# A last projection in two blocks of seven products

## The chip, the cores and the metric

One core of one Trainium2 chip runs the whole program. The metric is device time in microseconds (us) of one execution, lower being better. The profiled execution also has a span, from the first to the last instruction.

## The reference, cut to what matters

A two-layer decoder trunk on 512 rows of width 1024. Layer 1 is differential attention, layer 2 is a spatial gating unit of width 2048. Only the end of layer 2 and the final norm bear on the change:

```python
proj = h @ w_in                       # 512x1024 @ 1024x6144: u, v, gate
v = rms_norm(v, v_gain)
y = u * (W_s v + b) * silu(gate)      # 512 x 2048, causal 128x128 W_s per group
x = x + y @ sgu_w_out                 # 512x2048 @ 2048x1024   <- the change
return rms_norm(x, final_norm)
```

## The kernel before

Every large product is computed in three passes: each operand is split into a rounded part `hi` and a remainder `lo` (ScalarE makes `hi`, VectorE subtracts to make `lo`), and hi*hi, hi*lo and lo*hi are accumulated in PSUM.

Layer 2's input projection runs as six blocks, numbered 0 to 5. A block is 512x1024 times 1024x1024, done as a two by two block product in seven products instead of eight (Winograd's form of Strassen's scheme). The left operands (`sides`, seven pairs of hi and lo, 512 KB each in f32) come from the normed rows. The right operands come from four quarters a, b, c, d of the weights (1 MB each, tiles `quarter`): class `Quads` loads them with SyncE's queue (SP), splits them, and forms their sums on the way. Two sums are VectorE subtractions (L360, "b minus d" and "b minus a"), two are DMAs on GpSimd's queue (POOL) that add one quarter onto another: first c += a, then a += d. The second writes what the first reads, so it is issued only when the first has landed. The quarter forms are split two products ahead of their use, into three rotating buffer pairs `hi`, `lo` of the pool `wsp`. Call `quads.work(7*n+i+2)` does this during product i of block n.

Products are numbered 0 to 6. Products 0, 2, 4, 5 accumulate in the two banks `px`, products 1, 3, 6 in the two banks `py`. `product_n` (rows on the output partitions) has 24 matmuls of 512 columns; `product_t` (transposed output) has 48 of 256 columns. Blocks 0 and 1 use `product_n`, blocks 2 to 5 `product_t`. Block 5, the last, multiplies its result into `yT`, the layer's branch output (`times`, L993 and L999); after product 4 ScalarE copies `px` aside (`hold`), since product 5 accumulates on.

After block 5 the projection back is a plain product: `out_half` runs twice, once per 512 output columns, over 16 blocks of 128 in the contraction, 4 row blocks and 3 passes, 384 matmuls of 512 columns in all. Its weights come as eight chunks through `load` and `split` (L112, L129, L130), its left operand is split anew in each half (L267, L268). `residual` adds each finished row block onto the residual rows `xr` (L413) and squares it; `emit` computes the row scale by a Newton iteration, scales and stores. The sum of the last row block, its Newton iteration, scaling and store form the tail.

The program is scheduled at build time: each engine gets a fixed list of instructions, run in order; an engine whose next instruction waits does nothing else. `issue_after` pins some of them.

Of the kernel before, what the change touches and what calls it, by code (L numbers as in the profile page):

```python
# [2 lines left out]

# [1 line left out]

# [45 lines left out]
def build(ctx, tc, x, rel_bias, attn_norm, w_in, lq1, lk1, lq2, lk2, subln, w_out,  # L51
# [14 lines left out]
    def bank(name):  # L66
        return psum.tile([P, S], F32, tag="ps", name=name)
# [5 lines left out]
    def wide_src(w, c, n0):  # L73
        return w[0, c * S:(c + 1) * S, n0:n0 + S].rearrange("(k p) n -> p k n", p=P), [4, S]
# [18 lines left out]
        for c in range(4):  # L93
            chunks.append(wide_src(w_out, c, m * S))
    sgu_at = len(chunks)
    for m in range(2):
        for c in range(4):
            chunks.append(wide_src(sgu_w_out, c, m * S))

    raws, splits = {}, {}  # L100
    limit = [qk_first]
# [99 lines left out]
    def square(r, b, m=None):  # L201

        sl = slice(0, D) if m is None else slice(m * S, (m + 1) * S)
        c = 0 if m is None else m
        drop = yT[:, 10:12, :].rearrange("p k n -> p (k n)") if m is None else junk
        nc.scalar.activation(drop, xr[:, b, sl], AF.Square, accum_out=sq[r][b][:, c:c + 1])
        if c == 0:
            hv[r][b] = const.tile([P, 1], F32, name=f"hv{r}_{b}")

    def row_scale(r, b, halves):  # L210

        rs = small.tile([P, 1], F32, name="rs")
        if halves:
            nc.vector.scalar_tensor_tensor(hv[r][b], sq[r][b][:, 1:2], -0.5 / D, hv[r][b], ALU.mult, ALU.add)
        else:
            half_mean(r, b)
        newton(rs, hv[r][b], 1)
        return rs

    def half_mean(r, b):  # L220
        nc.vector.tensor_scalar(hv[r][b], sq[r][b][:, 0:1], -0.5 / D, -0.5 * EPS, ALU.mult, ALU.add)

    hi_last, hT_last, xs_last = [None], [None], [None]

# [286 lines left out]
    def columns_of(w, n0):  # L511
        def of(name):
            r, c = divmod("abcd".index(name), 2)
            return wide_src(w, r, n0 + c * S)[0]
        return of
# [284 lines left out]
        return [yp.tile([P, 4, S], F32R, tag=t, name=t) for t in ("yh", "yl")]  # L800

    acc = [bank(f"acc{b}") for b in range(NB)]
    quads = Quads(qp, [columns_of(sgu_w_in, n0) for n0 in columns])
# [49 lines left out]


    wst = sp.tile([P, KB, P], F32, name="wst")
    bs_bc = sp.tile([P, KB // 2 * P], F32, name="bs_bc")

    def spread_bias(m):
        src = sgu_b_s.rearrange("o g t -> o (g t)")[:, m * KB // 2 * P:(m + 1) * KB // 2 * P]
# [45 lines left out]
            nc.vector.tensor_tensor(v, of_bank(ps[i]), v, ALU.add)  # L905
            total(v, acc)

    i0 += 8
    assert i0 == sgu_at
    late = []  # L910
    for n in range(BR // D):
        for i in range(7):
# [86 lines left out]
            nc.vector.tensor_tensor(y, v.rearrange("p (j n) -> p j n", n=H), y, ALU.mult)  # L999

    VB = BR // D
    for m in range(2):
        for gates in (True, False):
            n = VB + 2 * m + (not gates)
            final = m == 1 and not gates
            t1 = temp()
            if final:
                t4, t2 = temp(), temp()
            for i in range(7):
                work = quads.work(7 * n + i + 2)  # L1010
                if final and i == 5:
                    limit[0] = len(chunks)
                    load(i0)
                if final and i > 4:
                    work = (split(i0, 2 * (i - 5) + h) for h in range(2))
# [12 lines left out]
                if i == (2 if m == 0 and gates else 1):  # L1028
                    times(gates, m, 0, 0, py, t1)
                if i == 2:  # L1030
                    t2 = t2 if final else temp()
                    hold(t2, px)
                if i == 4:
                    t4 = t4 if final else temp()
                    hold(t4, px)
                    times(gates, m, 1, 1, py, t4)
                if i == 5:
                    times(gates, m, 1, 0, px, temp() if gates else None, False)
                if i == 6:
# [4 lines left out]
    yps = tc.tile_pool(name="yp2", bufs=2)
    yp = yps.__enter__()
    fin = yp.tile([P, D], F32, name="fin", bufs=1)
    nc.scalar.dma_start(fin, final_norm.rearrange("(o d) -> o d", o=1).broadcast_to([P, D]))
    acc = [bank(f"acc{b}") for b in range(NB)]
    run(out_half(i0, 0, hT_store, range(4), acc, residual(2, 0, acc)))
    for b in range(NB):  # L1050
        nc.vector.tensor_tensor(xr[:, b, 0:S], xr[:, b, 0:S], fin[:, 0:S], ALU.mult)
    ov = out[0].rearrange("(b p) d -> p b d", p=P)
    acc = [bank(f"acc{b}") for b in range(NB)]
    last = residual(2, 1, acc)

    def emit(b):
        rs = row_scale(2, b, True)
        nc.scalar.activation(xr[:, b, 0:S], xr[:, b, 0:S], AF.Copy, scale=rs)
        nc.vector.scalar_tensor_tensor(xr[:, b, S:D], xr[:, b, S:D], rs, fin[:, S:D], ALU.mult, ALU.mult)
        for m in range(2):  # L1060
            nc.sync.dma_start(ov[:, b, m * S:(m + 1) * S], xr[:, b, m * S:(m + 1) * S])

    def finish(b):
        add = last(b)
        if b < NB - 2:
            emit(b)
        elif b == NB - 1:
            emit(b - 1)
            with tc.issue_after(add.ins):
                emit(b)  # L1070
# [25 lines left out]
```

## Time and profile before

| what | value |
|---|---|
| device time, median of 3 runs | 912.2 us (909.39 to 914.59) |
| device time of the profiled execution | 909.98 us |
| its span | 908.2 us |
| TensorE busy (PE) | 885.3 us, 97% of the span |
| VectorE busy (DVE) | 645.3 us, 71% |
| ScalarE busy (ACT) | 476.9 us, 53% |
| the chain of work that ended last | PE 82%, DVE 10%, DMA 3%, ACT 3%, issue 1% |
| mean granted TensorE clock | 0.997 of full speed |

Busy time of PE counts pipelined matmuls, so the step from one start to the next says what a matmul costs. DMA times run from issue to landing.

### The profile page before, as it was taken

Reading aid. Unit: us, or ns where it says so; the run is one execution under the profiler, and the core shown is the slowest. Engines: PE = TensorE matmul, PEld = TensorE weight load, DVE = VectorE, ACT = ScalarE, POOL = GpSimd, SP = SyncE. Lnnn points to the kernel's source line nnn. Section 1 sums busy time; section 2 is a strip of 40 time slices with the busy share of each in tenths; the row PEclk is TensorE's granted clock in tenths of the full one; section 3 lists DMA queues with packets and bytes.
Section 4 is the critical chain, followed back from the end, with each engine's and each line's share of the span. In section 5 each row is a group of like instructions: output and inputs, shape, how many; then the busy total and the mean of one; then the engine's idle time right before and its main releaser. Section 6 shows DMA issues by size and latency. Waiting matters only on the chain.

```text
span 908.2 us, 14110 instructions
## 1 busy us (share of the span) xinstructions
PE 885.3 (97%) x5393; PEld 774.6 (85%) x5393; DVE 645.3 (71%) x1399; ACT 476.9 (53%) x1015; POOL 34.4 (4%) x52
## 2 busy tenths in 40 slices
PE   7999999999999999999999999998999999999996
PEld 5878999988888888888788887787999999998884
DVE  6945665447787788688886839857795878685634
ACT  7634555446565565566664526736453444454532
POOL 0000100000000000000000002000100000000000
PEclk9999999999999999999999999999999999999998
DMA  8637755373222332321312615554656464534202
GB/s 286 234 90 210 206 192 105 116 245 95 78 90 83 103 90 83 103 89 40 105 47 82 243 29 131 188 128 151 139 163 139 141 139 140 117 134 149 86 4 93
DMA packets 55828, 115.48 MB, mean 127 GB/s; under 512 B 3965, under 2 KB 20398, under 8 KB 52432
## 3 DMA queue, kind: packets, MB, share of 16 engines
q1 hardware_dynamic: 49120, 79.70, 26.5%
q0 software_dynamic: 5584, 33.56, 15.5%
q10 hardware_dynamic: 1056, 1.32, 0.4%
q8 instruction: 42, 0.69, 0.3%
q14 instruction: 26, 0.21, 0.1%
HBM read 89.36 MB, written 6.33 MB: 105 GB/s over the span
## 4 chain that ended last, share of the span: by engine, by line
PE 82%; DVE 10%; DMA 3%; ACT 3%; issue 1%; SPq 0%; ACTq 0%; DVEq 0%; POOLq 0%
PE px L319 15%; PE py L319 11%; PE psqk L254 6%; PE psqk L256 6%; PE psqk L255 6%; PE acc L273 5%; PE acc L275 5%; PE acc L274 5%; PE psv L480 5%; PE po L732 3%; PE pss L694 3%; DMA quarter<-quarter 2%; PE pa L721 2%; DVE lo L374 2%; PE psy L981 2%; PE px L307 1%
## 5 line engine op out<-in xcount | busy, mean ns | idle before, releaser
L374 DVE TENSOR_TENSOR lo<-quarter,hi 128x1024 fp32r<-128x1024 f32 x126 | 152.8, 1236 | 86.0 <-ACT hi L373 85.6
L373 ACT CAST hi<-quarter 128x1024 fp32r<-128x1024 f32 x126 | 128.9, 1047 | 125.7 <-DMA quarter<-quarter 45.7
L130 DVE TENSOR_TENSOR lo<-raw,hi 128x512 fp32r<-128x512 f32 x144 | 93.5, 687 | 39.4 <-ACT hi L129 39.3
L129 ACT CAST hi<-raw 128x512 fp32r<-128x512 f32 x144 | 81.8, 620 | 54.9 <-PE psqk L255 24.7
L254 PE MATMUL psqk<-hT,hi 128*128 128x512 f32 x256 | 101.7, 397 | 0.0
L256 PE MATMUL psqk<-hT,lo 128*128 128x512 f32 x256 | 99.9, 390 | 0.0
L255 PE MATMUL psqk<-hT,hi 128*128 128x512 f32 x256 | 99.9, 390 | 0.0
L707 ACT ACTIVATE e<-e,nm 128x384 f32<-128x384 f32 (+3 forms) x128 | 70.8, 554 | 47.7 <-DVE nm L704 47.3
L319 PE MATMUL py<-hT,hi 128*128 128x256 f32 x512 | 93.0, 284 | 0.0
L273 PE MATMUL acc<-hi,hT 128*128 128x512 f32 x224 | 88.2, 394 | 0.5 <-DVE on L666 0.5
L274 PE MATMUL acc<-lo,hT 128*128 128x512 f32 x224 | 87.3, 390 | 0.0
L275 PE MATMUL acc<-hi,hT 128*128 128x512 f32 x224 | 87.0, 390 | 0.0
L319 PEld LDWEIGHTS py<-hT,hi 128*128 128x128 f32 x512 | 79.8, 192 | 0.0
L319 PE MATMUL py<-hT,lo 128*128 128x256 f32 x256 | 72.5, 283 | 0.0
L704 DVE CUSTOM_DVE_ANT_0 e<-pss,bias 128x384 f32<-128x384 f32 (+3 forms) x128 | 57.3, 484 | 4.1 <-PE pss L694 3.9
L254 PEld LDWEIGHTS psqk<-hT,hi 128*128 128x128 f32 x256 | 48.1, 188 | 12.9 <-issue 2.6
L268 DVE TENSOR_TENSOR hT<-yT,hT 128x512 fp32r<-128x512 f32 x56 | 37.0, 690 | 29.8 <-PE acc L274 17.4
L256 PEld LDWEIGHTS psqk<-hT,lo 128*128 128x128 f32 x256 | 48.1, 188 | 10.1
L255 PEld LDWEIGHTS psqk<-hT,hi 128*128 128x128 f32 x256 | 48.1, 188 | 9.4
L267 ACT CAST hT<-yT 128x512 fp32r<-128x512 f32 x56 | 33.5, 621 | 41.1 <-PE acc L274 35.2
L360 DVE TENSOR_TENSOR quarter<-quarter 128x1024 f32<-128x1024 f32 x36 | 43.3, 1222 | 11.5 <-DMA quarter<-in_sgu_w_in 10.8
L273 PEld LDWEIGHTS acc<-hi,hT 128*128 128x128 f32 x224 | 42.1, 188 | 10.5 <-issue 1.6
(218 smaller groups left out, 2026.6 us busy)
## 6 DMA issues: line engine op xcount, KB each, us to landing
quarter<-in_sgu_w_in SPq DMA_DIRECT2D x48, 512.0 KB, 5.4
raw<-in_attn_w_in SPq DMA_DIRECT2D x38, 512.0 KB, 4.6
quarter<-quarter POOLq DMA_DIRECT2D x18, 1024.0 KB, 7.5
quarter<-in_attn_w_in SPq DMA_DIRECT2D x24, 512.0 KB, 4.8
raw<-in_attn_w_out SPq DMA_DIRECT2D x16, 512.0 KB, 4.4
raw<-in_sgu_w_out SPq DMA_DIRECT2D x16, 512.0 KB, 4.3
vd<-yT POOLq DMA_DIRECT2D x4, 1024.0 KB, 6.0
v<-vd POOLq DMA_DIRECT2D x4, 1024.0 KB, 5.1
```

Of the source, the lines that this page charges most:

```text
L129: nc.scalar.copy(hi[:, sl], raw)
L130: nc.vector.tensor_tensor(lo[:, sl], raw, hi[:, sl].bitcast(F32), ALU.subtract)
L254: nc.tensor.matmul(ps, lhsT=w.hi[:, k, cs], rhs=hT[0][:, k, :], start=(k == 0), stop=False)
L255: nc.tensor.matmul(ps, lhsT=w.hi[:, k, cs], rhs=hT[1][:, k, :], start=False, stop=False)
L256: nc.tensor.matmul(ps, lhsT=w.lo[:, k, cs], rhs=hT[0][:, k, :], start=False, stop=(k == KD - 1))
L273: nc.tensor.matmul(acc[b], lhsT=yh[:, j, bs], rhs=w.hi[:, j, :], start=(k == 0), stop=False)
L274: nc.tensor.matmul(acc[b], lhsT=yh[:, j, bs], rhs=w.lo[:, j, :], start=False, stop=False)
L275: nc.tensor.matmul(acc[b], lhsT=yl[:, j, bs], rhs=w.hi[:, j, :], start=False, stop=(k == KB - 1))
L319: nc.tensor.matmul(ps[f // 2][:, f % 2 * H:(f % 2 + 1) * H], lhsT=w[x][:, k, f * P:(f + 1) * P], rhs=a[y][:, k, :], start=clear, stop=(k = ...
L373: nc.scalar.copy(hi[:, sl], raw[:, sl])
L374: nc.vector.tensor_tensor(lo[:, sl], raw[:, sl], hi[:, sl].bitcast(F32), ALU.subtract)
L707: nc.scalar.activation(e[f][:, cs], e[f][:, cs], AF.Exp, scale=-1.0, bias=nm[:, col], accum_out=l[:, col])
```

## The change

The plain projection is taken out. Its weights become two more blocks of `Quads`, numbered 6 and 7, one for each half of the contraction. Each is seven `product_n`. Their left operands are made from quarters y11, y12, y21, y22 of `yT` into the same buffers `sides`, as soon as the block before has used them (`left`); two sums there are VectorE subtractions and two are POOL DMAs of 512 KB. The results are added onto `xr`: five of the seven products by VectorE (`onto`), and `px` after products 0 and 2 by ScalarE copies and a POOL DMA that accumulates (`put_onto`). The final norm's squares are taken as the halves finish.

```diff
-    for m in range(2):
-        for c in range(4):
-            chunks.append(wide_src(sgu_w_out, c, m * S))
...
+    blocks = [columns_of(sgu_w_in, n0) for n0 in columns] + [rows_of(sgu_w_out, kb) for kb in range(2)]
+    quads = Quads(qp, blocks)
...
+    def left(kb, i):
+        y11, y12, y21, y22 = (quarter_of(kb, q, half) for half in range(2) for q in range(2))
+        raw = (y11, y12, y11, None, y21, y12, y22)[i]
+        if i == 3:
+            raw = temp().rearrange("p f n -> p (f n)").rearrange("p (k n) -> p k n", n=H)
+            nc.vector.tensor_tensor(raw, y21, y11, ALU.subtract)
+            nc.gpsimd.dma_start(y21, y22, accum_op=ALU.add)
+            yield
+        if i == 2:
+            nc.vector.tensor_tensor(y11, y11, y21, ALU.subtract)
+            nc.gpsimd.dma_start(y12, y11, accum_op=ALU.add)
+            yield
+        part(*sides[i], raw)
+        yield
+    def left_work(kb, i):
+        for j in ([], [0], [1], [], [3], [2], [4])[i]:
+            yield from left(kb, j)
+    def left_rest(kb, i):
+        for j in ([5], [], [6], [], [], [], [])[i]:
+            yield from left(kb, j)
...
             for i in range(7):
                 work = quads.work(7 * n + i + 2)
+                if n == OUT - 1:
+                    work = chain(work, left_work(0, i))
...
+    def onto(c, half, ps):
+        ms = slice(c * S, (c + 1) * S)
+        return [nc.vector.tensor_tensor(xr[:, b, ms], ps[b % 2], xr[:, b, ms], ALU.add)
+                for b in (2 * half, 2 * half + 1)]
+    def put_onto(c, half, ps):
+        t = temp()
+        hold(t, ps)
+        region = xr[:, 2 * half:2 * half + 2, c * S:(c + 1) * S]
+        nc.gpsimd.dma_start(region, t, accum_op=ALU.add)
...
+    for kb in range(2):
+        n = OUT + kb
+        for i in range(7):
+            work = chain(quads.work(7 * n + i + 2), left_rest(kb, i), left_work(1, i) if kb == 0 else ())
+            beside(product_n(py if i in (1, 3, 6) else px, sides[i], quads.forms[n, i], i in (0, 1, 3)), work)
+            if i == 0:
+                put_onto(0, 0, px)
+            if i == 1:
+                onto(0, 0, py)
+                if kb:
+                    first_half(0, 0)
+            if i == 2:
+                put_onto(0, 1, px)
+            if i == 3:
+                onto(1, 1, py)
+            if i == 4:
+                onto(1, 1, px)
+                if kb:
+                    first_half(1, 1)
+            if i == 5:
+                onto(1, 0, px)
+                if kb:
+                    for b in range(2):
+                        emit(b, 1)
+            if i == 6:
+                adds = onto(0, 1, py)
+                if kb:
+                    emit(2, 0)
+                    with tc.issue_after(adds[1].ins):
+                        emit(3, 0)
```

`first_half` squares a finished half row block and multiplies it by the norm's weights; `emit` is as before, with the half that finishes last as a parameter.

## Rows read from the trace of the kernel before

**Rows 1.** Busy times in windows: block 1, block 5, projection back (PE, PEld, DVE, ACT, POOL).
```profile
594.40:638.00 43.60, 41.07 (x186) 33.20 (x186) 28.56 (x30) 23.49 (x40) 1.74 (x2) 1.00 0.54 145
772.40:812.50 40.10, 40.10 (x338) 40.10 (x337) 28.51 (x37) 20.36 (x30) 1.70 (x2) 1.00 0.46 120
812.50:899.40 86.90, 86.90 (x385) 71.81 (x383) 47.21 (x92) 35.65 (x69) 0.00 (x0) 1.00 0.24 79
```

**Rows 2.** PE's waits, 555 to 910 us: total, times, longest.
```profile
PE px L307 <- ACT yT L897: 2.8, 3, 1.7
```

**Rows 3.** Timeline of PE (start, duration): projection's first and last matmul, product starts.
```profile
812.36 0.40 PE L273 MATMUL acc<-hi,hT 128*128 128x512 f32 x1
...
899.20 0.39 PE L275 MATMUL acc<-hi,hT 128*128 128x512 f32 x1
...
800.93 0.28 PE L319 MATMUL px<-s4h,hi 128*128 128x256 f32 x1
```

**Rows 4.** Timeline of PE in block 1: products 0, 2, 4 and 5.
```profile
594.44 0.39 PE L307 MATMUL px<-hi,hT 128*128 128x512 f32 x1
...
606.00 0.39 PE L308 MATMUL px<-lo,s2h 128*128 128x512 f32 x1
...
611.13 0.40 PE L309 MATMUL px<-hi,s2l 128*128 128x512 f32 x1
...
618.67 0.50 PE L307 MATMUL px<-hi,s1h 128*128 128x512 f32 x1 [0.79 <-ACT yT L897]
...
629.51 0.50 PE L307 MATMUL px<-hi,s4h 128*128 128x512 f32 x1 [1.74 <-ACT yT L897]
```

**Rows 5.** Timeline of DVE around the end of block 4: wide and narrow steps.
```profile
766.87 2.36 DVE L360 TENSOR_TENSOR quarter<-quarter 128x1024 f32<-128x1024 f32 x2
769.14 0.69 DVE L999 TENSOR_TENSOR yT<-raw,yT 128x512 f32<-128x512 f32 x1
769.74 2.36 DVE L374 TENSOR_TENSOR lo<-quarter,hi 128x1024 fp32r<-128x1024 f32 x2
```

**Rows 6.** DVE by line in block 5, 772.4 to 812.5 us.
```profile
L374 DVE TENSOR_TENSOR lo<-quarter,hi 128x1024 fp32r<-128x1024 f32 x10 | 12.1, 1223 | 6.4 <-ACT hi L373 6.4
...
L130 DVE TENSOR_TENSOR lo<-raw,hi 128x512 fp32r<-128x512 f32 x6 | 4.0, 688 | 0.6 <-ACT hi L129 0.5
L268 DVE TENSOR_TENSOR hT<-yT,hT 128x512 fp32r<-128x512 f32 x5 | 3.4, 687 | 1.1 <-ACT hT L267 1.1
```

**Rows 7.** Timeline of DVE, products 4 and 5 of block 5.
```profile
802.36 0.68 DVE L130 TENSOR_TENSOR lo<-raw,hi 128x512 fp32r<-128x512 f32 x1
802.96 0.69 DVE L999 TENSOR_TENSOR yT<-raw,yT 128x512 f32<-128x512 f32 x1
```

**Rows 8.** Timeline of POOL: the accumulating DMAs of blocks 1 and 5.
```profile
595.96 0.87 POOL L365 DMA_DIRECT2D quarter<-quarter  x1 [33.36 <-ACT hi L373]
604.17 0.87 POOL L365 DMA_DIRECT2D quarter<-quarter  x1 [7.34 <-DVE lo L374]
...
772.40 0.85 POOL L365 DMA_DIRECT2D quarter<-quarter  x1 [35.24 <-DVE lo L374]
780.31 0.85 POOL L365 DMA_DIRECT2D quarter<-quarter  x1 [7.06 <-issue]
```

**Rows 9.** Timeline of ACT: what it did when the second accumulating DMA landed.
```profile
615.53 1.05 ACT L373 CAST hi<-quarter 128x1024 fp32r<-128x1024 f32 x1 [10.10 <-DMA quarter<-quarter]
616.49 0.63 ACT L900 ACTIVATE junk<-yT 128x512 f32<-128x512 f32 x1
...
788.00 2.00 ACT L373 CAST hi<-quarter 128x1024 fp32r<-128x1024 f32 x2 [7.38 <-DMA quarter<-quarter]
```

**Rows 10.** Timeline of DVE in block 1: a sum, and the split after the landing.
```profile
605.52 0.69 DVE L905 TENSOR_TENSOR yT<-py,yT 128x512 f32<-128x512 f32 x1 [0.92 <-PE py L309]
...
616.61 1.22 DVE L374 TENSOR_TENSOR lo<-quarter,hi 128x1024 fp32r<-128x1024 f32 x1 [9.80 <-ACT hi L373]
```

**Rows 11.** All 18 accumulating DMAs of L365, 1 MB each.
```profile
DMA to landing us min/median/max: 6.9/7.5/11.3
```

**Rows 12.** Timeline of DVE: last sum onto the rows and last scaling.
```profile
900.33 0.68 DVE L413 TENSOR_TENSOR xr<-acc,xr 128x512 f32<-128x512 f32 x1
...
903.59 0.75 DVE L1059 SCALAR_TENSOR_TENSOR xr<-xr,rs,fin 128x512 f32<-128x512 f32 x1
```

More of the change, by code (lines that the diff above doesn't have):

```diff
@@ L2 @@
 from contextlib import ExitStack
+from itertools import chain
 import numpy as np
@@ L206, in square, with row_scale @@
         nc.scalar.activation(drop, xr[:, b, sl], AF.Square, accum_out=sq[r][b][:, c:c + 1])
-        if c == 0:
+        if b not in hv[r]:
             hv[r][b] = const.tile([P, 1], F32, name=f"hv{r}_{b}")
-    def row_scale(r, b, halves):
+    def row_scale(r, b, halves, second=1):
         rs = small.tile([P, 1], F32, name="rs")
         if halves:
-            nc.vector.scalar_tensor_tensor(hv[r][b], sq[r][b][:, 1:2], -0.5 / D, hv[r][b], ALU.mult, ALU.add)
+            nc.vector.scalar_tensor_tensor(hv[r][b], sq[r][b][:, second:second + 1], -0.5 / D, hv[r][b], ALU.mult,
+                                           ALU.add)
         else:
@@ L218, in row_scale, with half_mean @@
         return rs
-    def half_mean(r, b):
-        nc.vector.tensor_scalar(hv[r][b], sq[r][b][:, 0:1], -0.5 / D, -0.5 * EPS, ALU.mult, ALU.add)
+    def half_mean(r, b, m=0):
+        nc.vector.tensor_scalar(hv[r][b], sq[r][b][:, m:m + 1], -0.5 / D, -0.5 * EPS, ALU.mult, ALU.add)
     hi_last, hT_last, xs_last = [None], [None], [None]
@@ L802, in build, with rows_of, of @@
     acc = [bank(f"acc{b}") for b in range(NB)]
-    quads = Quads(qp, [columns_of(sgu_w_in, n0) for n0 in columns])
+    def rows_of(w, kb):
+        def of(name):
+            r, c = divmod("abcd".index(name), 2)
+            return wide_src(w, 2 * kb + r, c * S)[0]
+        return of
+    blocks = [columns_of(sgu_w_in, n0) for n0 in columns] + [rows_of(sgu_w_out, kb) for kb in range(2)]
+    quads = Quads(qp, blocks)
     gen = out_half(i0 + 4, 1, lambda c: (hT_store if c < 2 else yp_store)(c), range(4), acc,
@@ L855, in build @@
     wst = sp.tile([P, KB, P], F32, name="wst")
-    bs_bc = sp.tile([P, KB // 2 * P], F32, name="bs_bc")
+    bs_bc = sp.tile([P, KB // 2 * P], F32, tag="row", name="bs_bc")
     def spread_bias(m):
@@ L906, in plus @@
             total(v, acc)
-    i0 += 8
-    assert i0 == sgu_at
+    assert i0 + 8 == sgu_at
     late = []
@@ L1001, in build, with quarter_of @@
     VB = BR // D
+    OUT = 3 * VB
+    def quarter_of(kb, q, half):
+        return yT[:, 8 * kb + 4 * q:8 * kb + 4 * q + 4, half * H:(half + 1) * H]
+    def left(kb, i):
[18 more added lines that the diff above has]
+            yield from left(kb, j)
     for m in range(2):
@@ L1004, in build @@
             n = VB + 2 * m + (not gates)
-            final = m == 1 and not gates
             t1 = temp()
-            if final:
-                t4, t2 = temp(), temp()
             for i in range(7):
                 work = quads.work(7 * n + i + 2)
[L1011 to L1015, printed above, removed]
+                if n == OUT - 1:
+                    work = chain(work, left_work(0, i))
                 beside(product_t(py if i in (1, 3, 6) else px, sides[i], quads.forms[n, i], i in (0, 1, 3)), work)
@@ L1030, in build @@
                 if i == 2:
-                    t2 = t2 if final else temp()
+                    t2 = temp()
                     hold(t2, px)
                 if i == 4:
-                    t4 = t4 if final else temp()
+                    t4 = temp()
                     hold(t4, px)
@@ L1040, in build @@
                     times(gates, m, 0, 1, py, t2)
+    fin = sp.tile([P, D], F32, tag="row", name="fin")
+    nc.scalar.dma_start(fin, final_norm.rearrange("(o d) -> o d", o=1).broadcast_to([P, D]))
+    ov = out[0].rearrange("(b p) d -> p b d", p=P)
+    def onto(c, half, ps):
[7 more added lines that the diff above has]
+        nc.gpsimd.dma_start(region, t, accum_op=ALU.add)
@@ new lines, in first_half, with emit @@
+    def first_half(m, half):
+        ms = slice(m * S, (m + 1) * S)
+        for b in (2 * half, 2 * half + 1):
+            square(2, b, m)
+            half_mean(2, b, m)
+            nc.vector.tensor_tensor(xr[:, b, ms], xr[:, b, ms], fin[:, ms], ALU.mult)
+    def emit(b, m):
+        square(2, b, m)
+        rs = row_scale(2, b, True, m)
+        o, n = slice((1 - m) * S, (2 - m) * S), slice(m * S, (m + 1) * S)
+        nc.scalar.activation(xr[:, b, o], xr[:, b, o], AF.Copy, scale=rs)
+        nc.vector.scalar_tensor_tensor(xr[:, b, n], xr[:, b, n], rs, fin[:, n], ALU.mult, ALU.mult)
+        for sl in (o, n):
+            nc.sync.dma_start(ov[:, b, sl], xr[:, b, sl])
@@ L1041, in build @@
     scope.__exit__(None, None, None)
     quarters.__exit__(None, None, None)
[L1044 to L1070, printed above, removed]
@@ L1072, in build @@
-    run(out_half(i0 + 4, 1, hT_store, range(4), acc, finish))
-    yps.__exit__(None, None, None)
 _INS = ["x", "rel_bias", "attn_norm", "attn_w_in", "attn_lam_q1", "attn_lam_k1", "attn_lam_q2", "attn_lam_k2",
```

## The prediction

> **What bounds the kernel now.** I read the windows first [rows 1]: in block 5 and in the projection back PE is busy without a gap, at full granted clock, while DVE has 28.5 of 40.1 us and 47.2 of 86.9 us. So at this end of the kernel only fewer matmuls help. Next the list of PE's waits [rows 2]: from 555 us on its longest total is 2.8 us, and every line in it is a `product_n` line of blocks 0 and 1; no `product_t` of blocks 2 to 5 and no matmul of the projection waits. Block 1 is the only steady block of the kind that the change builds, and there PE has 41.1 of 43.6 us. The timelines of PE, POOL, ACT and DVE say why, and the argument stands on them.
>
> **What is removed.** 384 matmuls become 2 x 7 x 24 = 336. The price of one is the step between starts, not its 390 ns: (899.20 - 812.36) / 383 = 0.2267 us [rows 3]. 48 x 0.2267 = **10.9 us saved**. Against it, the products whose side lies in a tile of sums step slower: 22 steps from 606.00 to 611.13 are 0.233 us each [rows 4]. Three of seven products are such: 2 x 72 x 0.0065 = **0.9 us back**.
>
> **What is added off PE.** A wide VectorE operation (128x1024) costs 1.135 us back to back (766.87 to 769.14 for two), a narrow one 0.6 [rows 5]. Block 5 loses 11 narrow ones (L130, L268) [rows 6] and gets 15 wide: two splits of block 6 (4), its subtractions (4), sides 0, 1, 3, 2, 4 (5 remainders, 2 subtractions). 28.5 - 6.6 + 17.0 = 38.9 of 40.1 us. Block 6 has 14 + 4 + 9 wide and 10 narrow operations, 30.6 + 6.0 = 36.6 us in 7 x 5.45 = 38.2 us. So VectorE fits, at 96 to 97%, but only without waiting, and in block 5 its splits alone wait 6.4 us for ACT [rows 6]. I charge nothing for these operations by themselves; their cover is PE's time, and what they cost is lateness, worked out below. ScalarE has room (20.4 us in block 5). The 16 weight loads of 512 KB stay on SP, now into quarters as these come free; the `fin` load stays on ACT's queue, behind nothing new. POOL gets twelve new DMAs: four of 1 MB (quarters), eight of 512 KB (sides and `put_onto`).
>
> **Where PE will wait.** Time 0 is the start of block 6 (812.36). Each block carries c += a, then a += d, then the split for product 4. In block 5 the first was issued at +0.1 after the block's start (772.40; the start is 772.3, seven products of 5.72 us before 812.36), in block 1 at +1.5 [rows 4, 8].
>
> Block 6: VectorE reaches product 5 of block 5 with its `times` free at 803.56, less the one L130 that falls away: -9.4 [rows 7]. Then in its list: split (6,0) 2.3, b - d 2.3, side 2 2.3, `times` 1.2, split (6,1) and b - a 4.5. So c += a is issued at **+3.1**. From one issue to the next it was 8.2 us in block 1 and 7.9 in block 5; the second landed 11.4 us after its issue in block 1, where weight loads ran beside it, and 7.7 in block 5 [rows 8, 9]. All 18 lie between 6.9 and 11.3 [rows 11]. Loads for block 7 run here too: I take 8.2 and 9.5. `put_onto` puts 512 KB into the same queue; the trace has no such transfer, so between 0 and half of 7.5 us, and I take 1, since it is issued when much of c += a has moved. Landing L = 3.1 + 8.2 + 9.5 + 1 = 21.8 (18.3 to 26.4). In block 1 product 4 started 3.1 us after the landing (615.53 to 618.67): 24.9, against 4 x 5.45 + 0.3 = 22.1 due. **2.8 us (0 to 7.4).**
>
> Then product 5 of block 6. It accumulates on `px`, which VectorE must first add onto the rows, behind everything that stood behind the landing: 1.1 to the first remainder [rows 9, 10], split (6,4) 2.3, split (6,5) 2.3, the add of `py` 1.2, split (6,6) 2.3, y21 - y11 1.1, then 0.6 for the first bank: L + 10.9. Product 4 ends at L + 3.1 + 5.45. **2.3 us** (0 if the add goes first; 4.6 if two sides stand there too). Before, a ScalarE copy freed `px` at this point and PE went straight on (800.93 [rows 3]); in block 1, PE waited 1.74 us within product 5 [rows 4].
>
> Block 7: from product 5 of block 6 the list is 1.1 + 0.6 + 2.3 + 2.3 + 2.3 + 1.2 + 4.5 = 14.3 us in 10.9, so c += a is at +3.4. No weights load any more: 3.4 + 7.9 + 7.7 + 1 = 20.0 (18.6 to 23.1), product 4 at 23.1: **1.0 us (0 to 4.1)**. Product 5: as above without y21 - y11, L + 9.8 against L + 8.55: **1.2 us (0 to 3.5)**.
>
> The tail stays: the last bank is added, put through Newton and scaled with the same operations (900.33 to 903.59 [rows 12]), and the banks of the last four row blocks finish 8.2, 5.4, 2.7 and 0 us before the last matmul, as now. Bound: 0.5 us either way, taken as 0.
>
> A 1 MB accumulating DMA takes 7.5 us in the median here [rows 11]. The Trainium skill ("DMA: Bandwidth & Descriptors", section on the anatomy of one DMA on the software path) fits 2.0 us plus bytes over 436 GB/s, which would be an estimated 4.4 us. By it the chain would land at about +12 and neither product 4 would wait, about 7 us better than my sum; the trace disagrees with it for accumulating transfers, so I keep the rows.
>
> **Sum.** -10.9 + 0.9 + (2.8 + 2.3 + 1.0 + 1.2) = -2.7 us. The profiled execution took 909.98 us (span 908.2), so 907.3; the median of the runs is 2.2 above it, so **909.5**. With all waits at their low ends -10.0, at their high ends +9.6. The measurement tells 0.5%, 4.6 us, from no change.
>
> **The rivals.**
> *The chain lands in time (faster).* If VectorE is not late at the end of block 5, c += a goes out at +0.1; with 7.5 and 7.7 us it lands at 15.3, VectorE never stands and none of the four waits appears: -10.0, 902.2. For it: blocks 2 to 5 have the same chain and PE never waits. Against it: there a product takes 5.72 us and not 5.45, and VectorE had room; in block 1 the chain landed at +21.1.
>
> *`put_onto` queues behind the second quarter DMA (slower).* POOL's list is fixed at build. If a += d stands ahead of `put_onto` of product 0, POOL waits for c += a to land, and `put_onto` is issued at 3.1 + 8.2 + 0.9 and lands behind a += d: + 9.5 + 3.8 = 25.5. VectorE's add of `py` waits for that, since both add to the same rows, and product 3 (due at 16.5) needs `py`: 9.6 us; then 2.3 at product 5. In block 7, 3.4 + 7.9 + 0.9 + 7.7 + 3.8 = 23.7, 7.8 us, and 1.2. Together 20.9, so +10.9: 923; with the quicker landings of both 917. It decides if a += d is listed first: `put_onto` is ready at 6.0, a += d only when c += a has landed, but lists made as though DMAs were quick put it first. For it: ACT stood 10.1 us before a split that waited for this very DMA, with a square behind it whose input was ready at 606.2 and which ran at 616.49 [rows 9, 10]. Against it: a += d also needs split (6,2), which VectorE has at about +9.
>
> **How the numbers follow.** My forecast, PE's saving mostly eaten by waits (5.4 to 14.6 us of them), 0.40; its own range is 907.6 to 916.8. The chain in time or nearly so, 902 to 907.6, 0.36: it is well supported by four blocks, and the lateness that I charge is small beside the uncertainty of a fixed order that I infer. Behind the queue, or the waits near their high ends, 0.24. Hence faster 0.36, same 0.40, slower 0.24. The range leaves out about 1 in 10 at each side: 903 to 917.
>
> **What would show it.** PE in blocks 6 and 7: gaps of 1 to 3 us at the starts of products 4 and 5 and none elsewhere. POOL: c += a issued 3 us after each block's start, and `put_onto` before a += d. VectorE: above 90% busy from 772 us on. The matmul step 0.227 to 0.233. I am wrong if c += a goes out near 0 (then faster), if PE stands at the start of product 3 (slower), or if the tail from the last matmul is not 8.8 us.

## The result, and the profile after

The changed kernel takes 924.49 us (median of 4 runs, 921.91 to 927.16), beside 912.29 us for the kernel before on the same chip: a ratio of 1.0136, 95% interval [1.009, 1.0181]. It is slower, and above the range that was given (903 to 917, predicted 909.5). The profiled execution took 922.71 us, with a span of 921.0 us against 908.2.

First where the span grew. These are the windows of the changed kernel, cut at the starts of block 5, 6 and 7 and at the last matmul; the columns are those of [rows 1].

```profile
772.30:821.40 49.10, 42.65 (x338) 42.44 (x337) 35.87 (x38) 23.47 (x28) 4.30 (x4) 0.93 0.63 151
821.40:872.40 51.00, 42.68 (x170) 33.80 (x169) 36.61 (x39) 22.57 (x25) 6.75 (x6) 0.90 0.72 165
872.40:911.80 39.40, 38.86 (x169) 31.28 (x168) 30.79 (x53) 18.61 (x31) 4.20 (x4) 1.00 0.46 94
```

Block 5, whose own matmuls are not changed, takes 49.1 us where it took 40.1 [rows 1]: 9.0 us lost before the new work has begun on TensorE. Block 6 takes 51.0 and block 7 39.4. Together these two take 90.4 us for 87.1 of the plain projection (812.36 to 899.43 [rows 3]): 3.3 us lost. The tail grew by 0.45 us. VectorE, forecast at 96 to 97%, is busy for 36 of 49 and 37 of 51 us.

PE's waits over the same stretch (total, times, longest), which had no entry at all there before [rows 2]:

```profile
PE px L318 <- ACT raw L331: 6.5, 1, 6.5
PE py L306 <- ACT hi L372: 5.1, 1, 5.1
PE px L306 <- DVE xr L1078: 2.7, 2, 2.1
PE py L307 <- DVE lo L373: 1.1, 1, 1.1
```

Together 15.4 us. PE's timeline has them at these places (start, duration):

```profile
807.54 0.58 PE L318 MATMUL px<-s4h,hi 128*128 128x256 f32 x1 [6.45 <-ACT raw L331]
807.92 0.42 PE L318 MATMUL px<-s4l,hi 128*128 128x256 f32 x1
808.14 0.41 PE L318 MATMUL px<-s4h,lo 128*128 128x256 f32 x1
...
812.94 0.28 PE L318 MATMUL px<-s4l,hi 128*128 128x256 f32 x1
813.06 0.28 PE L318 MATMUL px<-s4h,lo 128*128 128x256 f32 x1
...
843.21 0.77 PE L306 MATMUL py<-hi,hT 128*128 128x512 f32 x1 [5.13 <-ACT hi L372]
...
860.43 0.68 PE L306 MATMUL px<-hi,s4h 128*128 128x512 f32 x1 [2.14 <-DVE xr L1078]
```

The rows are product 5 of block 5, product 3 and product 5 of block 6. Block 7 has one wait, of 0.5 us, at product 5. The second to fifth row show what each longer stand costs beside itself: the step after it is 0.22 us and only later 0.12. The row of product 3 names a cast of ScalarE's, which ended at 843.2 and is not an operand of that product; VectorE's add of `py` onto the rows, which frees the bank that product 3 writes, ran from 842.37 (below), its first bank 0.69 us. Four windows of PE (busy, granted clock, DMA share, GB/s) say why the steps are slow: one before the stand, and one behind each of the three stands.

```profile
794.00:801.00 7.00, 7.00 (x60) 1.00 0.98 217
807.50:812.60 5.10, 5.06 (x23) 0.50 0.85 244
843.20:848.50 5.30, 5.29 (x16) 0.65 0.84 186
860.40:864.00 3.60, 3.57 (x9) 0.53 1.08 201
```

Behind the first stand the granted clock is 0.50, the lower of its two levels (1.2 GHz); the last two windows reach past the end of that stretch, and show 0.65 and 0.53. Product 5 of block 5 took 8.12 us for 5.68, and product 3 of block 6 took 7.32 for 5.45. So the three longer stands cost 13.7 us by themselves and some 2 us more each.

What came late? ScalarE behind product 4 of block 5, where `hold` (L331) has to free `px`:

```profile
803.13 1.05 ACT L297 CAST s2h<-yT 128x1024 fp32r<-128x1024 f32 x1 [8.90 <-DVE yT L1022]
804.08 1.99 ACT L372 CAST hi<-quarter 128x1024 fp32r<-128x1024 f32 x2
805.97 1.04 ACT L297 CAST hT<-raw 128x1024 fp32r<-128x1024 f32 x1
806.92 0.57 ACT L331 COPY raw<-px 128x512 f32<-128x512 f32 x1
```

Side 2 of block 6 stands ahead of `hold` in ScalarE's list, and it waits 8.9 us for VectorE's y11 - y21 (L1022). VectorE's timeline shows what that waited for, and the same kind of wait at four other places:

```profile
789.50 1.23 DVE L373 TENSOR_TENSOR lo<-quarter,hi 128x1024 fp32r<-128x1024 f32 x1 [4.55 <-ACT hi L372]
...
801.87 1.23 DVE L1022 TENSOR_TENSOR yT<-yT 128x1024 f32<-128x1024 f32 x1 [4.87 <-DMA yT<-yT]
...
842.37 1.29 DVE L1078 TENSOR_TENSOR xr<-py,xr 128x512 f32<-128x512 f32 x2 [7.24 <-DMA xr<-raw]
...
855.14 1.22 DVE L1022 TENSOR_TENSOR yT<-yT 128x1024 f32<-128x1024 f32 x1 [3.73 <-DMA yT<-yT]
...
884.94 0.69 DVE L1078 TENSOR_TENSOR xr<-py,xr 128x512 f32<-128x512 f32 x1 [2.63 <-DMA xr<-raw]
...
913.09 0.68 DVE L1078 TENSOR_TENSOR xr<-py,xr 128x512 f32<-128x512 f32 x1
...
916.36 0.75 DVE L1100 SCALAR_TENSOR_TENSOR xr<-xr,rs,fin 128x512 f32<-128x512 f32 x1
```

The last two rows are the tail, which runs as before [rows 12]. POOL's timeline has the issues (against [rows 8]):

```profile
780.19 0.86 POOL L364 DMA_DIRECT2D quarter<-quarter  x1 [6.82 <-issue]
795.41 1.29 POOL L1019 DMA_DIRECT2D yT<-yT  x1 [14.37 <-PE py L318]
...
822.13 0.89 POOL L364 DMA_DIRECT2D quarter<-quarter  x1 [17.20 <-DVE quarter L359]
...
830.31 0.86 POOL L364 DMA_DIRECT2D quarter<-quarter  x1 [7.28 <-issue]
830.86 1.53 POOL L1085 DMA_DIRECT2D xr<-raw  x1
...
879.05 1.20 POOL L1085 DMA_DIRECT2D xr<-raw  x1 [3.29 <-ACT raw L331]
882.46 0.91 POOL L364 DMA_DIRECT2D quarter<-quarter  x1 [2.21 <-DVE lo L373]
```

Read with VectorE's rows: y21 += y22 (L1019) is issued at 795.41, and L1022, which reads y21, goes on at 801.87, 6.5 us later. In block 6, c += a is issued 0.7 us after the block's start, a += d at 830.31, and `put_onto` right behind it. VectorE's add of `py` onto the same rows goes on at 842.37, 11.5 us after that. In block 7 the order is the other way round, and VectorE goes on 5.9 us after `put_onto`'s issue. The medians from issue to landing, over the whole run (against [rows 11]):

```profile
quarter<-quarter POOLq DMA_DIRECT2D x22, 1024.0 KB, 7.6
...
yT<-yT POOLq DMA_DIRECT2D x4, 512.0 KB, 6.4
xr<-raw POOLq DMA_DIRECT2D x4, 512.0 KB, 5.4
```

Half the bytes take 5.4 to 6.4 us, not half the time.

### The profile page after: what moved, and what is told of

Read it like the earlier page. It is cut to its first block, busy times and chain, and to the rows that moved or that the text cites. A ratio compares the mean times of both kernels' runs of the same rounds, so it can differ in the third digit from the quotient of the medians.

```text
span 921.0 us, 14023 instructions
## 1 busy us (share of the span) xinstructions
PE 882.3 (96%) x5345; PEld 769.6 (84%) x5345; DVE 673.3 (73%) x1401; ACT 486.1 (53%) x1001; POOL 48.2 (5%) x64
## 5 line engine op out<-in xcount | busy, mean ns | idle before, releaser
L373 DVE TENSOR_TENSOR lo<-quarter,hi 128x1024 fp32r<-128x1024 f32 x154 | 186.0, 1233 | 91.4 <-ACT hi L372 91.0
L372 ACT CAST hi<-quarter 128x1024 fp32r<-128x1024 f32 x154 | 156.8, 1047 | 146.0 <-DMA quarter<-quarter 50.8
L128 DVE TENSOR_TENSOR lo<-raw,hi 128x512 fp32r<-128x512 f32 x112 | 73.0, 688 | 39.0 <-ACT hi L127 39.0
L127 ACT CAST hi<-raw 128x512 fp32r<-128x512 f32 x112 | 64.0, 621 | 48.4 <-PE psqk L254 24.8
L359 DVE TENSOR_TENSOR quarter<-quarter 128x1024 f32<-128x1024 f32 x44 | 52.9, 1221 | 9.6 <-DMA quarter<-in_sgu_w_in 9.4
L253 PEld LDWEIGHTS psqk<-hT,hi 128*128 128x128 f32 x256 | 48.1, 188 | 12.8 <-issue 2.6
L255 PEld LDWEIGHTS psqk<-hT,lo 128*128 128x128 f32 x256 | 48.1, 188 | 10.1
L306 PE MATMUL py<-hi,hT 128*128 128x512 f32 x112 | 44.8, 400 | 5.8 <-ACT hi L372 5.1
L318 PEld LDWEIGHTS py<-hT,lo 128*128 128x128 f32 x256 | 49.1, 192 | 0.0
L307 PE MATMUL py<-lo,hT 128*128 128x512 f32 x112 | 44.5, 397 | 1.1 <-DVE lo L373 1.1
L308 PE MATMUL py<-hi,hT 128*128 128x512 f32 x112 | 44.5, 397 | 0.0
L479 PE MATMUL psv<-hi,hT 128*128 128x512 f32 x128 | 41.8, 404 | 0.5 <-ACT hT L240 0.5
L364 POOL DMA_DIRECT2D quarter<-quarter x22 | 19.5, 888 | 397.6 <-DVE lo L373 216.1
```

What stands on the lines that cost most here:

```text
L127: nc.scalar.copy(hi[:, sl], raw)
L128: nc.vector.tensor_tensor(lo[:, sl], raw, hi[:, sl].bitcast(F32), ALU.subtract)
L253: nc.tensor.matmul(ps, lhsT=w.hi[:, k, cs], rhs=hT[0][:, k, :], start=(k == 0), stop=False)
L255: nc.tensor.matmul(ps, lhsT=w.lo[:, k, cs], rhs=hT[0][:, k, :], start=False, stop=(k == KD - 1))
L306: nc.tensor.matmul(ps[i], lhsT=a[0][:, k, rs], rhs=w[0][:, k, :], start=(start and k == 0), stop=False, **more)
L318: nc.tensor.matmul(ps[f // 2][:, f % 2 * H:(f % 2 + 1) * H], lhsT=w[x][:, k, f * P:(f + 1) * P], rhs=a[y][:, k, :], start=clear, stop=(k = ...
```

## Experiments

Two theories were tried against each other. By the first (A, called A2 and A3 in later runs, as each expectation states it), the loss is engines that stand in a fixed list for a DMA, the work queued behind them, and the slow clock behind each stand of PE. By the second (B), the loss is that VectorE has no room for the new work. "The kernel" below is the changed one; times are medians, ratios are to the kernel before, run beside it. Rows and block times are those of the one profiled execution, and diffs are cut to the line that matters.

**Which DMA.** The two sums of the left sides, or `put_onto` of `px`, or both, become VectorE adds.

```diff
-            nc.gpsimd.dma_start(y21, y22, accum_op=ALU.add)
+            nc.vector.tensor_tensor(y21, y21, y22, ALU.add)
...
-            nc.gpsimd.dma_start(y12, y11, accum_op=ALU.add)
+            nc.vector.tensor_tensor(y12, y12, y11, ALU.add)
```

> The two POOL DMAs of each block's left sums (y21 += y22, y12 += y11) become VectorE additions, four wide operations of 1.14 us more in all. Theory A (an instruction that waits for a POOL DMA stands in VectorE's and ScalarE's fixed lists ahead of the add or copy that frees px): the 6.45 us gap at product 5 of block 5 and its slow matmuls (2.4 us) go, and so does most of the 5.4 us lost in products 5 and 6 of block 6; the 5.1 us gap at product 3 of block 6 stays, since it belongs to the sum onto the rows. 14 us less than the changed kernel: 908 to 912 us. Theory B (VectorE is full, 96%, and its lateness is what PE waits for): 4.6 us more work on VectorE, so no gain or a loss, 922 to 929 us.

917.87 us, 1.0056 [1.0037, 1.0074]: 6.6 us of the 12 come back, but in the profiled execution not in block 5. It still takes 49.1 us, while the loss at products 5 and 6 of block 6 is gone (45.9 us). PE's first wait there:

```profile
PE px L318 <- ACT raw L331: 6.6, 2, 6.0
```

The list order (side 2 and a split ahead of `hold`) is unchanged, and the chain of the quarters was later in this run: a += d, issued at 784.03 beside the weight loads of block 6, had ScalarE waiting until 794.80, 10.8 us. So block 5 has two sources of lateness that feed one list, and taking one away left the other. In the changed kernel's profile the same DMA let ScalarE go on 8.2 us after its issue (780.19 to 788.42). The profiled execution of e1, though, is the longest of ten (920.95), and PE had stood 1.3 us in block 4 already, which the edit does not touch; no profile shows block 5 in a shorter one. The plain form of theory A, one wait behind one gap, did not come out here.

```diff
-                put_onto(0, 0, px)
+                onto(0, 0, px)
...
-                put_onto(0, 1, px)
+                onto(0, 1, px)
```

> px of products 0 and 2 is added onto the rows by VectorE instead of a ScalarE copy and a POOL DMA, eight narrow operations of 0.6 us more on VectorE. Theory A: only the gap at product 3 of block 6 (5.1 us and 1.9 us of slow matmuls) goes, the gap at product 5 of block 5 stays: 915 to 919 us. Theory B: 4.8 us more on VectorE, 922 to 929 us.

924.04 us, 1.0095 [1.0063, 1.0127]. The gap at product 3 of block 6 goes (block 6 43.0 us), but block 5's gap grows to 9.7 and block 7 takes 44.1. This profile too is of the longest of seven executions (926.82; three took 918.3 to 918.6), in which ScalarE again went on 10.8 us after the issue of a += d.

> Both of the above. Theory A: all three losses go, 20 us less than the changed kernel, 902 to 906 us, faster than the kernel before. Theory B: 9.4 us more VectorE work, 925 to 934 us.

918.33 us, 1.0059 [1.0031, 1.0088]. Block 6 42.2, but block 5 50.1 with a gap of 6.0, and block 7 44.6 with waits for VectorE at products 1, 4 and 5. The profile is of the longest of eight executions (924.97; five took 915.4 to 919.7); here ScalarE went on 11.1 us after a += d's issue. In it each wait removed is partly given back by another.

**An earlier issue.** y21 - y11 and the DMA behind it move from product 4 to product 1.

```diff
-        for j in ([], [0], [1], [], [3], [2], [4])[i]:
+        for j in ([], [3, 0], [1], [], [3], [2], [4])[i]:
```

> The same work as the changed kernel on every engine, but y21 - y11 and the DMA y21 += y22 are issued in product 1 instead of product 4; only the remainder and cast of side 3 stay in product 4. Theory A: the DMA has landed long before its sum is wanted, so the gap at product 5 of block 5 and the wait for y21 in block 6 go: 908 to 913 us. Theory B: VectorE's work is the same, so the time is that of the changed kernel, 921 to 927 us.

924.13 us, 1.0118 [1.0094, 1.0141]. Block 5 falls to 44.8 us, its gap to 2.6 (now within product 4), so this DMA is indeed part of its loss. It was issued 14.4 us earlier in the block, 0.6 us behind a += d, and VectorE went on only 6.7 us earlier, after a wait of 10.3. Block 6 gets a gap of 10.75 at product 3: there the early DMA is issued at 834.16, right behind a += d (832.90) and `put_onto` (833.45), and three transfers are in flight on the queue at once.

**The order of the lists.** `issue_after` pins the work of product 5 behind `hold` (block 5) and behind VectorE's add of `px` (blocks 6 and 7); nothing else changes.

```diff
-                beside(product_t(...), work)
+                with tc.issue_after(freed[0].ins) if n == OUT - 1 and i == 5 else ExitStack():
+                    beside(product_t(...), work)
```

> The same operations, transfers and sizes as the changed kernel; only the lists' order differs: ScalarE's work of product 5 in block 5 is put behind the copy of px of product 4, and VectorE's work of product 5 in blocks 6 and 7 behind the add of px of product 4. With that the sum of px onto the rows also comes ahead of the second quarter DMA in POOL's list of block 6. Theory A2 (the order of the lists is at fault: work that belongs to product 5 stands ahead of the copy that frees px, and put_onto behind a DMA that waits 8 us): block 5 falls from 49.1 us to 41 to 43, the gap at product 3 of block 6 (5.1 us and 1.9 us of slow matmuls) goes, and what is left in block 6 is the wait at product 4 for the two quarter DMAs, some 3 us. In all 906 to 914 us. Theory B (VectorE's and POOL's amount of work sets the pace): the work is the same, so the wait moves to another product: 920 to 927 us.

924.87 us, 1.0126 [1.0079, 1.0172]. Block 5 falls to 43.0 us and the gap at its product 5 is gone, which shows that the list order carries that gap. The time does not move: PE now stands 2.15, 3.71 and 2.3 us in block 6, each time with a product of about 7.2 us behind it, and block 7 takes 43.6 us.

> Only POOL's list is changed: in blocks 6 and 7 the sum of px of product 0 onto the rows is issued before the second quarter DMA. Theory A2: the gap at product 3 of block 6 (7 us with its slow matmuls) becomes a shorter one at product 4, since the quarter DMA now comes later (3 us); block 5 stays at 49 us: 918 to 922 us. Theory B: no change, 921 to 927 us.

Here POOL's list has `put_onto` of product 0 ahead of a += d:

```diff
-                put_onto(0, 0, px)
+                put = put_onto(0, 0, px)
+                with tc.issue_after(put.ins):
+                    quads.add(n, "a", "d")
```

927.25 us, 1.0154 [1.0123, 1.0186]. The gap at product 3 is gone, so the queue order made it; but later VectorE stands for the left side's sum with everything behind it, and PE for VectorE at product 6. The row of VectorE, with its wait:

```profile
858.56 1.22 DVE L1022 TENSOR_TENSOR yT<-yT 128x1024 f32<-128x1024 f32 x1 [9.97 <-DMA yT<-yT]
```

PE's gap behind it is 11.74 us, the longest of all runs.

**Pins with one kind of DMA gone.**

> The pins of e5_pin, and the left sums by VectorE instead of POOL (four wide operations, 4.6 us, more on VectorE). Theory A2: block 5 as in e5_pin, and no instruction waits for a 512 KB sum of the left side any more; the loss of 5.4 us in products 5 and 6 of block 6 goes as it did in e1_left_dve: 904 to 911 us. Theory B: 4.6 us more than e5_pin.

917.23 us, 1.0045 [1.0012, 1.0078]: as without the pins (e1), within the intervals.

> The pins of e5_pin, and px of products 0 and 2 added onto the rows by VectorE (eight narrow operations, 4.8 us, more on VectorE; no DMA onto the rows). Theory A2: no product waits for a DMA onto the rows, 2 to 4 us less than e5_pin: 904 to 911 us. Theory B: up to 4.8 us more than e5_pin.

916.61 us, 1.0051 [1.0007, 1.0095]. With the gap of block 5 and `put_onto` out of the way, the longest wait left is at the place that the prediction worked out, product 4 of block 6, with a partner in block 7:

```profile
PE px L306 <- DVE xr L1081: 4.0, 1, 4.0
...
PE px L306 <- ACT hi L373: 1.9, 1, 1.9
```

c += a went out 5.6 us after the block's start, a += d 7.6 us later, and ScalarE went on behind its landing at +21.5. But what PE waited for is VectorE's add of `px` after product 2, which this run itself put into VectorE's list behind the split that waited for the landing. By the prediction's own 3.1 us from landing to start, product 4 would have stood some 0.6 us.

**All the new DMAs, one kind, or VectorE's work left out.** e9 drops the twelve new accumulating DMAs, e10 those of blocks 6 and 7's quarters alone, e11 the fourteen remainders of the left sides. The diff is e11's.

```diff
-        part(*sides[i], raw)
+        nc.scalar.copy(sides[i][0], raw)
```

> Leaves out all twelve new accumulating DMAs: the quarter sums of blocks 6 and 7, the two left sums of each, and the sums of px of products 0 and 2 onto the rows. PE, ScalarE and VectorE keep every instruction. Theory A3 (waits for POOL DMAs, in whichever order the lists stand, make nearly all of PE's gaps): blocks 5 to 7 fall from 139.4 us to 118 to 124 us, PE's work alone being 117: 901 to 909 us, faster than the kernel before. Theory B (VectorE has 96% of the time to fill, so any order leaves PE waiting for it): VectorE's work is the same, blocks 5 to 7 stay above 132 us: 915 to 924 us.

904.38 us, 0.992 [0.9891, 0.9949]. Its blocks 5, 6 and 7, in windows as above:

```profile
773.00:813.00 40.00, 40.00 (x338) 40.00 (x337) 32.73 (x36) 23.61 (x28) 1.70 (x2) 1.00 0.58 159
813.00:855.30 42.30, 40.71 (x170) 32.53 (x170) 40.49 (x42) 22.68 (x25) 0.00 (x0) 0.96 0.28 100
855.30:894.10 38.80, 38.77 (x169) 31.35 (x168) 30.32 (x55) 19.21 (x31) 0.00 (x0) 1.00 0.04 14
```

All the work of PE, ScalarE and VectorE is there, in the same list order in block 5 (side 2 is still cast ahead of `hold`), and block 5 takes its 40.0 us without a gap. VectorE has 40.5 of 42.3 us in block 6 and PE waits 1.6 us in all. In block 5 c += a and a += d are still DMAs, and VectorE still waits 4.53 us for the split behind them; only the left sides' DMAs are gone there. So with the new DMAs gone the order does no harm, VectorE's work fits (103.5 us in the three blocks, for 103.3 in the changed kernel), and the loss comes from these DMAs: from the waits for them, by the rows above, though this run takes their traffic away too.

> Leaves out only the four quarter DMAs of 1 MB in blocks 6 and 7. Theory A3: put_onto has POOL's queue to itself, the gap at product 3 of block 6 goes (7 us with its slow matmuls), block 5 keeps its gap of 6.4 us, and products 5 and 6 of block 6 keep their wait for y21: 914 to 919 us. Theory B: 921 to 927 us.

922.41 us, 1.0129 [1.0077, 1.0181]: the chain of the quarters alone is not it. Block 5 keeps its gap (6.4), the one at product 3 of block 6 goes, and PE stands 6.2 us for VectorE at product 6 of block 6, where VectorE waits 8.6 us for y21 += y22.

> Leaves out VectorE's fourteen remainders of the left sides (15.9 us of its work, in blocks 5, 6 and 7); the matmuls read old values. All DMAs and ScalarE casts stay. Theory A3: the gap at product 5 of block 5 stays (it waits for the DMA y21 += y22) and so does the one at product 3 of block 6: 915 to 922 us. Theory B: with 16 us less for VectorE the gaps go: 902 to 910 us.

921.81 us, 1.0118 [1.0083, 1.0153]. Taking 15.9 us of work from VectorE moves the ratio by 0.002; gaps of 4.7, 4.6 and 3.4 us remain, and VectorE is busy for 92.5 of 140 us. Theory B falls, as the cause of this kernel's loss. It falls by e9 and e11, and not by the ranges as such: A's ranges came out in e9 and e11 alone so far, the times of e2, e4, e5 and e10 lie in B's, and those of e1, e3, e6, e7 and e8 in neither, since A took each cure to be worth a whole gap and another wait took its place.

**A version without the waits.** VectorE adds c += a in blocks 5 to 7 (below), y21 += y22 (not in e14), and `px` onto the rows after product 0 (in e12 and e14 after product 2 as well), with the pins of e5. As DMAs stay y12 += y11, a += d, and in e13 one `put_onto` for each block.

```diff
-                self.add(n, "c", "a")
+                for h in range(2):
+                    sl = slice(2 * h, 2 * h + 2)
+                    nc.vector.tensor_tensor(c[:, sl], c[:, sl], a[:, sl], ALU.add)
```

> The pins, and four kinds of POOL DMA replaced by VectorE operations so that none of them stands in front of a fixed list: y21 += y22 of each half (2 wide operations in all), px of products 0 and 2 onto the rows (8 narrow), and the first quarter sum c += a of blocks 5, 6 and 7 (6 wide), so that the second, a += d, is issued at once and no longer 8 us later. 13.8 us more for VectorE. The same result as the reference. Theory A3: blocks 5 to 7 at 119 to 126 us against 133.4 with the pins and the sums of px on VectorE alone: 900 to 908 us. Theory B, or that the pins were not the cause: VectorE has 123 us of work for 117 us of PE: 914 us or more.

914.51 us, 1.0019 [1.0, 1.0037]. Block 5 is 40.05 us, but the time lies in theory B's range, and so does the next run's.

> As e12_chain, but px of product 2 goes onto the rows by ScalarE and a POOL DMA, since nothing reads those rows before product 6: 2.4 us less for VectorE, two more DMAs of 512 KB. Theory A3: within 2 us of e12_chain, or better by up to 2 us: 899 to 908 us. Theory B: 912 us or more.

913.31 us, 1.0009 [0.9991, 1.0026].

> As e12_chain, but y21 += y22 stays a POOL DMA. It tells the quarter chain from the left sums. Theory A3: VectorE waits 4 to 5 us for y21 in block 5 and as long in block 6; some 4 to 8 us more than e12_chain: 905 to 914 us. If it is no slower than e12_chain, the left sums cost nothing once the quarter chain is short.

915.95 us, 1.0029 [1.0014, 1.0044], not to be told from e12: with c += a quick and the pins in place, what the wait for y21 costs is within the noise, and not the 4 to 8 us that were expected. e13's ratio is 1.0009 for 1.0136, with the same products: eleven of the twelve microseconds came back with these waits, but none of the saving is left over, since the adds are now VectorE's work. What PE stands for now is VectorE, at product 1 of block 7 in e13 for 4.1 us, with the two halves of c += a listed ahead of the add that frees `py`. The next two move these adds behind it, with the pins and without.

> As e13_chain_p0 (blocks 40.1, 43.9, 45 us; 913.3 us), but in blocks 6 and 7 VectorE's two adds of c += a are listed behind the add that frees py in product 0, not ahead of it. Theory A2 (what is left over the saving is PE standing for work that waits in an engine's list behind other work, and the slow product after each longer stand): the gap of 4.14 us at product 1 of block 7 and the 1.9 us of its slow product go, and the 1.79 us at product 1 of block 6: 7.8 us less, 905 to 907 against a before of about 912. Rival (VectorE has no slack left in these blocks, so that lateness moved in one place comes back in the next): the gaps come back at products 3 to 5, and the time stays at 912 to 914.

911.36 us, 0.9984 [0.9969, 0.9999]: below the rival's range by 0.6 us and far above A2's.

> As e15_late_c without the pins (the sides and splits of product 5's successors may stand ahead of the step that frees px). Theory A2: with nothing of VectorE's list waiting for a DMA the order does little harm: block 5 within 1 us of e15's, the whole within 3 us of e15. Rival (the order itself is what costs): block 5 has a gap of 2 us or more at product 5 and the whole is 4 us or more above e15.

910.51 us, 0.9985 [0.9972, 0.9998]. This is the best version: 14 us better than the changed kernel, and not to be told from the kernel before by the bound of 0.5%. Its windows, and PE's waits in them:

```profile
774.00:814.50 40.50, 40.36 (x339) 40.16 (x338) 36.98 (x39) 23.75 (x28) 2.13 (x2) 1.00 0.54 144
814.50:856.70 42.20, 39.34 (x171) 31.27 (x170) 39.37 (x43) 21.11 (x23) 2.73 (x3) 1.00 0.49 137
856.70:900.00 43.30, 39.43 (x169) 31.09 (x167) 37.80 (x61) 18.57 (x30) 2.69 (x3) 1.00 0.31 61
```

```profile
PE px L306 <- DVE xr L1090: 4.7, 4, 1.4
PE py L306 <- DVE xr L1090: 1.9, 1, 1.9
```

Every wait left is for VectorE's adds onto the rows, 6.6 us in five pieces, with VectorE busy for 39.4 of 42.2 and 37.8 of 43.3 us. So here the rival of e15 holds: lateness moved in one place comes back in the next. The pins are worth nothing once VectorE waits for no DMA, as in this run.

**The adds on GpSimd itself.** c += a, and in the second run the left sides' sums too, taken off VectorE and off the DMA queue.

```diff
-                nc.vector.tensor_tensor(c[:, sl], c[:, sl], a[:, sl], ALU.add)
+                nc.gpsimd.tensor_tensor(c[:, sl], c[:, sl], a[:, sl], ALU.add)
```

> As e16_late_c_nopin (blocks 40.5, 42.2 and about 43 us; 910.5 us), but the six halves of c += a in blocks 5 to 7 are adds on GpSimd itself, neither DMAs nor VectorE's work, listed in product 1 again. VectorE loses 6 x 1.135 = 6.8 us of 122 in 772 to 905. No row of these kernels shows such an add; the nearest, one pass of GpSimd over 128x2048, took 2.25 us, so one half costs between 1.1 and, if two operands cost twice that, 2.3 us. Theory A3 (without DMA waits what is left over is VectorE's fullness, 5 to 6 us in blocks 6 and 7): the gaps of 1.2 to 1.9 us at products 1, 2 and 5 shrink, the time is 906 to 909. Rival (GpSimd's adds come slower than 4 us for one half, or hold VectorE up while they run, so that the sum is late for a += d): gaps of 2 us or more at product 4 and 5, the time 911 to 916.

917.4 us, 1.0069 [1.0043, 1.0094].

> As e17_pool_c, but the sums of the left sides, y21 += y22 (on VectorE in e16) and y12 += y11 (a DMA in e16), are GpSimd's adds too. VectorE loses 3 x 1.135 us more and only a += d and one put_onto for each block stay as DMAs. Theory A3: 905 to 908, with block 5 at 40 us. Rival (GpSimd's adds are slow or hold VectorE up): block 5 above 41 us with a gap at product 5, the time 911 to 920.

923.8 us, 1.0125 [1.0099, 1.015]. GpSimd's adds in e17 as a group, and in e18 one of them in POOL's timeline with the VectorE step beside it:

```profile
L367 POOL TENSOR_TENSOR quarter<-quarter 128x1024 f32<-128x1024 f32 x6 | 21.6, 3618 | 52.8 <-DVE lo L380 32.1 <-DVE quarter L359 20.8
```

```profile
803.06 3.21 POOL L1033 TENSOR_TENSOR yT<-yT 128x1024 f32<-128x1024 f32 x1 [1.41 <-DVE yT L1032]
```

```profile
804.03 3.32 DVE L298 TENSOR_TENSOR s2l<-yT,s2h 128x1024 fp32r<-128x1024 f32 x1
```

One add takes 3.6 us in the mean of e17's six and 3.2 in e18's row, three times VectorE's 1.2, and VectorE's remainder of side 2, 1.23 us in the changed kernel, takes 3.32 beside it: it ends 1.1 us, its own length, after the add (807.35 and 806.27). The Trainium skill ("SBUF — State Buffer", section "Who interferes with whom") says that a VectorE instruction with two inputs in SBUF contends with a GpSimd instruction that reads SBUF; the slow step is of this kind, so the trace agrees there. More steps of that kind took 2.2 to 3.5 us beside other adds in both runs. Beside e18's first add they took their usual 1.2 us, but that add took 5.1 us and the one behind it 3.4. The rival held in both runs in kind; the times lie above even its ranges.

## Why the prediction was wrong, point by point

**The step that failed.** "I charge nothing for these operations by themselves; their cover is PE's time, and what they cost is lateness, worked out below" was worked out for one chain only, the quarters'. The four sums of left sides and two of the four `put_onto` were counted ("POOL gets twelve new DMAs") and given neither a landing time nor a waiter. Even the list worked out for c += a has "side 2 2.3" with no wait, though that step reads y21 after its DMA. The sum therefore had no term for block 5, which lost 9.05 us: VectorE stands for a += d (4.55) and for y21 += y22 (4.87), side 2's cast stands for VectorE, and `hold`, which frees `px`, stands behind that cast. The first of these waits was there before ([rows 6]: 6.4 us of such waits in all) and does no harm by itself: e9 keeps it (4.53) and has block 5 whole with the left sides' DMAs gone. In e1's profile, where it was 8.6 us, block 5 lost as much without the other. e5 takes only the order away, and the gap goes. [Rows 9], read for rival B alone, would have warned: ScalarE stood 10.1 us for a DMA with other work behind it.

**The choice between the forecast and rival B.** In block 6 POOL's list did have a += d ahead of `put_onto`, as the rival said, and PE stood at product 3 as it said, 5.1 us and not 9.6; c += a went out at +0.7 and not at +3.1, probably because PE's own stand in block 5 had let VectorE catch up (in e8, without that stand, it was +5.6). In block 7 the order was the forecast's. With the order turned (e6) the gap at product 3 went, and the time did not fall. I took 1 us for `put_onto`; where it queues it took 11.5 from issue to go-ahead.

**A term that was missing.** After the three longer stands PE ran on at the granted clock's lower level for 3.5 to 5 us, some 2 us each, 6 in all. No wait of mine carried it.

**What held.** The matmuls: blocks 6 and 7 of e9 take 42.3 and 38.8 us, and the latter, 38.6 from its first start to the end of its last step, twice would be 77.1 against 87.1, 10.0 us saved, as in -10.9 + 0.9. The wide VectorE step (1.14 us) and VectorE's share of block 6 (40.5 of 42.3 in e9, 96%, as forecast, though I had 36.6 us of work). The tail, +0.45 of 0.5. Block 7 came out better than forecast, 39.4 us against 38.1 + 0.45 + 2.2 = 40.8.

**What only looked right.** The four waits. Product 5 of block 6 waited 2.1 us where I had 2.3, but VectorE stood there for y21 += y22 (3.73) and not behind the landing of a += d; with that sum on VectorE (e1) the wait is gone. Product 4 waited in neither block: in block 6 product 3 had stood before it, in block 7 a += d was in at +17.7 (890.14) where I had 20.0. In e8 the landing is at +21.5 where I had 21.8, by chance: c += a later, the landings quicker, and no `put_onto` in the queue.

**The sum.** Forecast -2.7, found +12.8 in the span: block 5 +9.05, blocks 6 and 7 +3.3 where I had -2.7, tail +0.45.

**What stays open.** Whether some order lets VectorE carry the adds without PE waiting: e9, which leaves out their sums, is 6.5 us below the kernel before, and e16 gets 1.5. How much of the DMAs' lateness is queueing behind each other and how much sharing with the weight loads was not separated either. Which of e17's and e18's waits come from GpSimd's slowness and which from its hold on VectorE was not separated.

## What to carry to other kernels

For every new DMA write down who waits for it and what stands behind that waiter in its fixed list, also in the stage ahead of the change, where its cover is borrowed. Cost a gap of 2 us and more of a saturated TensorE as the gap and, in most cases here, some 2 us of slow matmuls behind it. When a wait is removed, look for the next one before counting the gain: here single cures gave back 0 to 7 us, and only three together gave back all 12.

## What the hardware showed unexpectedly

A stand of one length left the clock alone in one run and not in another. Product 1 of block 7 starts after 1.87 us in both e16 and e15; the timeline and the window behind it in e16:

```profile
864.16 0.47 PE L306 MATMUL py<-hi,hT 128*128 128x512 f32 x1 [1.87 <-DVE xr L1090]
```

```profile
864.20:869.00 4.80, 4.80 (x21) 1.00 0.00 0
```

and in e15:

```profile
866.57 0.59 PE L306 MATMUL py<-hi,hT 128*128 128x512 f32 x1 [1.87 <-DVE xr L1093]
```

```profile
866.60:870.50 3.90, 3.90 (x10) 0.56 0.00 0
```

In e11 even a stand of 3.42 us, at product 3 of block 6, left it alone: the product behind it took 5.57 us, at a granted clock of 1.00.

```profile
840.25 0.47 PE L306 MATMUL py<-hi,hT 128*128 128x512 f32 x1 [3.42 <-DVE xr L1078]
```

And a DMA that adds 512 KB within SBUF is not half of one that adds 1 MB: 5.4 and 6.4 us against 7.6, and 11.5 us behind a 1 MB one on the same queue.
